# A chunked scan layer: masks move from GpSimd to VectorE, the state copy to ScalarE, two groups of loads and transposes later

## The chip, the cores and the metric

The kernel runs on one core of a Trainium2 chip. The metric is the device time of one execution in microseconds, as the median of several runs. The engines are TensorE (PE; its weight loads are listed apart as PEld), VectorE (DVE), ScalarE (ACT), GpSimd (POOL) and SyncE (SP). SP and GpSimd issue the DMA transfers of this kernel, each in the order of its own queue.

## What is computed

One layer of a latent generator, on 1024 latent and 256 context tokens with 2048 channels, in fp32. The part that matters here is a two-directional recurrence with 16 heads of 64 channels:

```python
def _rwkv_step(S, inp):
    r, w, k, v, a, b = inp
    sa = jnp.einsum('dbhvk,dbhk->dbhv', S, a)
    S = S * w[..., None, :] + sa[..., :, None] * b[..., None, :] + v[..., :, None] * k[..., None, :]
    y = jnp.einsum('dbhvk,dbhk->dbhv', S, r)
    return S, y
...
p_l = h_l @ w_in[l]                       # one input projection for all branches
S_ctx, y_c = bidir_scan(S0, *cx)          # 256 context tokens
_, y_l = bidir_scan(S_ctx, *lat)          # 1024 latent tokens
out_l = branch_output(p_l, y_l, ...)      # per-head norm of y, gates, a pooling branch, output projection
x = x + gt_l * out_l
return rms_norm(x, final_g)
```

## The kernel before

The kernel has three stages. The first (0 to about 956 us in the profile) makes the modulation, the normalised input and those columns of the input projection that the scan needs; it writes the scan's operands to DRAM (sAR, sBK, sV, sBV). The second is the scan, with the rest of the input projection woven in. The third (from about 1993 us) is the output projection with residual and norm.

The scan runs in chunks of 64 tokens. There are four groups Q of four heads and 20 chunks each (4 of context with g = 0, 16 of latent tokens), so NST = 80 steps k, each with both directions of four heads. A chunk's recurrence is solved with a triangular inverse. A step has these parts:

- `scores` (L758) multiplies the chunk's operands on TensorE into two PSUM banks, 20 steps ahead (LEAD). `masked` (L762 to L773) multiplies them with a triangular mask into the SBUF tile NM and stores it to DRAM (sNM) from GpSimd's queue. ns is 1 for context chunks (256 columns a head) and 2 for latent ones (512).
- `inverse(i)` inverts the diagonal 32x32 blocks of eight steps at once: four loads of TT from sNM (L783), then 30 pairs of VectorE instructions (L789, L791), then a store. Its first `next`, in `begin`, issues the loads. `invert` then places the pairs among the other VectorE work, and at step r = k % 8 = 4 `run_step` runs whatever is left of the inversion.
- `assemble` builds the 64x64 inverses T from these blocks (L826, L837) with one PSUM bank, B0.
- `phase_x` (L893), `phase_t` (L903), `phase_s` (L915) are the serial chain of a step. Each ends in VectorE instructions that read PSUM: Xs (L896), two SUV copies (L904, L905), and for the state St (L918) and two halves of the next step's SUV (L922). The new state Sn (L923) is made on GpSimd; the next step's `outputs` (L935, L937) and phase_s read it.
- `turned` (L881) transposes the next step's BK into bank B0, and ScalarE copies it to BKt (L882).
- `gathered` collects the outputs y. When a pair of chunks is complete in both directions, `finish` normalises it (L972 to L985), loads its gates (sBV and sG), transposes it on TensorE into bank B0 (L1001) and writes it to sM.

Between these stand `unit`s of the input projection (12 matmuls of 512 columns, L154 to L156; planned as 2.65 us), which `pump` places, and generators (`threads`: weight splits L633, gate and pooling work, `finish`), which `slot` advances. The order on TensorE, VectorE and ScalarE is the order in which the code emits the instructions; SP and GpSimd are ordered by the framework. `at["pe"]` and `at["dve"]` are the planned times of the two engines: `slot` and `invert` place VectorE work as long as `at["dve"]` is below the time that they are given. A thread that yields 0 is left until the next call of `slot`; `later()` yields 0 until one more unit has been emitted. `dense[0]` is true between phase_s of a step and the first phase of the next.

Buffers around the scan: NM, R, MR, AR, S two each, NA and SUV three, BK four, one PSUM bank for each of XU, B0, A0 and A1.

Of the kernel before, what the change touches and what calls it, by code (L numbers as in the profile page):

```python
# [11 lines left out]
ALU = mybir.AluOpType  # L12
# [47 lines left out]
def hybrid_layer_kernel(ctx: ExitStack, tc: tile.TileContext, I, out, dbg=None):  # L60
# [496 lines left out]
    with ExitStack() as p2s:  # L557
# [200 lines left out]
                    mm(ps[h][:, 64 * ns * u:64 * ns * (u + 1)], BK[hs, u // 2, u % 2, :], AR[hs, :, u // 2, u % 2, :],  # L758
                       start=True, stop=True)

        def masked(k, direct=False):
            ns = 2 if steps[k][1] else 1  # L762
            ps = scps.pop(k)
            NM = p2.tile([128, ns, 2, 4 * C], F32, tag="NM", bufs=2, name=nm("NM"))
            for h in range(2):
                nv = NM[:, :, h].rearrange("q a (u t) -> q u a t", t=C)
                pv, mv = ps[h][:, 0:256 * ns].rearrange("q (u a t) -> q u a t", u=4, a=ns), mask[:, h, :, 0:ns, :]
                if direct:
                    V.tensor_tensor(nv, pv, mv, ALU.mult)
                else:  # L770
                    S.copy(nv, pv)  # L771
                    G.tensor_tensor(nv, nv, mv, ALU.mult)  # L772
            idma(sNM[0:ns, :, :, k].rearrange("a h q u t -> q (a h) (u t)"), NM.rearrange("q a h x -> q (a h) x"))  # L773


# [131 lines left out]
        def phase_s(k):  # L907
            Q, g, s = steps[k]
            c = CCH * g + s
            SUV, S0, DY = suv[k], st["S"], bank(("DY", "B1")[k % 2])  # L910
            if c < NCH - 1:
                BKt = bkts.pop(k)
                for u in range(4):
                    for h in range(2):
                        mm(DY[hss[h], 64 * u:64 * u + 64], BKt[:, u // 2, u % 2, h, :], SUV[:, h, u // 2, u % 2, :],  # L915
                           start=True, stop=True)
                tmp = p2.tile([128, 4, C], F32, tag="St", name=nm("St"))
                V.tensor_tensor(tmp.rearrange("q u v -> q (u v)"), DY[:, 0:256], S0.rearrange("q u v -> q (u v)"), ALU.add)  # L918
                Sn = p2.tile([128, 4, C], F32, tag="S", bufs=2, name=nm("S"))
                pc = PCt[:, Q, c].rearrange("q p d -> q (p d)").unsqueeze(2).broadcast_to([128, 4, C])  # L920
                for h in range(2):
                    V.tensor_tensor(suv[k + 1][hss[h], h].rearrange("q p d v -> q (p d) v"), tmp[hss[h]], pc[hss[h]], ALU.mult)  # L922
                G.tensor_tensor(Sn, tmp, pc, ALU.mult)  # L923
                st["S"] = Sn
            if g:
                st["late"] = k, S0, DY
            else:
                suv.pop(k)
# [37 lines left out]
        def finish(Q, m, y):  # L966
            runs = (C * (6 - 2 * m), C * (8 + 2 * m))
            js = slice(2 * Q, 2 * Q + 2)
            mean = p2.tile([128, 8], F32, tag="mean", bufs=2, name=nm("mean"))
            rs = p2.tile([128, 8], F32, tag="rs", bufs=2, name=nm("rs"))  # L970
            yf = y.rearrange("q p r c v -> q (p r c) v")
            V.tensor_reduce(mean, yf, mybir.AxisListType.X, ALU.add)  # L972
            V.tensor_scalar(mean, mean, 1.0 / C, None, op0=ALU.mult)
            yield 0.7
            V.tensor_tensor(yf, yf, mean.unsqueeze(2).broadcast_to([128, 8, C]), ALU.subtract)
            sq = p2.tile([128, 8, C], F32, tag="sqy", bufs=2, name=nm("sqy"))
            S.activation(sq, yf, AF.Square)
            yield 0.7
            yield from later()
            V.tensor_reduce(rs, sq, mybir.AxisListType.X, ALU.add)  # L980
            S.activation(rs, rs, AF.Sqrt, bias=eps_ln, scale=1.0 / C)
            yield 0.6
            yield from later()
            V.reciprocal(rs, rs)
            V.tensor_tensor(yf, yf, rs.unsqueeze(2).broadcast_to([128, 8, C]), ALU.mult)  # L985
            while gates_done[0] < 2 * Q + 2:
                unit()
            parts = []
            for src in (sBV, sG):
                t = p2.tile([128, 2, 2, 128], F32, tag="bvs", bufs=2 * BVS, name=nm("bvs"))  # L990
                for r in range(2):
                    dma(t[:, :, r], src[js, :, runs[r]:runs[r] + 128].rearrange("j q t -> q j t"))
                parts.append(t)
            yield 0.8
            yield 0
            while not dense[0] and not rush[0]:
                yield 0
            ps = bank("B0")
            for i in range(8):
                for h in range(2):  # L1000
                    mm(ps[hss[h], 64 * i:64 * i + 64], yf[hss[h], i, :], ident[hss[h], hss[h]], start=True, stop=True)  # L1001
            mx = p2.tile([128, 2, 2, 128], F32, tag="mxn", bufs=2, name=nm("mx"))
            for p in range(2):
                j = 2 * Q + p
                S.activation(mx[:, p].rearrange("q r t -> q (r t)"), ps[:, 256 * p:256 * p + 256], AF.Identity,
                             bias=lbs[:, j:j + 1], scale=lgs[:, j:j + 1])
            yield from later()
            V.tensor_tensor(mx, mx, parts[0], ALU.add)  # L1008
            yield 0.7
            V.tensor_tensor(mx, mx, parts[1], ALU.mult)  # L1010
            for r in range(2):
                idma(sM[js, :, runs[r]:runs[r] + 128].rearrange("j q t -> q j t"), mx[:, :, r])
            yield 0.7
# [22 lines left out]
        def run_step(k):  # L1036
            r = k % 8
            last = k == NST - 1
            phase_x(k)
            pe(0.7, st.get("suv", 0.0))  # L1040
            xs = dve(0.41, at["pe"])
            if r in (0, 5) and k // 4 + 1 < len(batches):
                asm["now"] = assemble(k // 4 + 1)
                next(asm["now"])
            late = st.pop("late", None)
            if late:
                outputs(*late)
                pe(1.7)
            else:
                unit()  # L1050
                owed[0] -= 1
            bk_load(k + 2)
            if not last:
                step_loads(k + 1)
            if k + LEAD + 2 < NST:
                score_loads(k + LEAD + 2)
            dense[0] = False
            invert(k, max(at["pe"], xs) + 0.5)
            slot(max(at["pe"], xs) + 0.4)
            phase_t(k)  # L1060
            pe(0.7, xs)
            us = dve(0.84, at["pe"])
            if late:
                gathered(*late)
                dve(0.56)
            if k + LEAD < NST:
                scores(k + LEAD)
                pe(1.7)
            elif unit_no[0] < NU:
                unit()  # L1070
                owed[0] -= 1
            if r in (2, 7) and "now" in asm:
                run(asm.pop("now"))
                pe(0.6)
            invert(k, max(at["pe"], us) + 0.5)
            slot(max(at["pe"], us) + 0.4)
            dense[0] = True
            phase_s(k)
            pe(0.7, us)
            st["suv"] = dve(1.48, at["pe"])  # L1080
            if not last:
                turned(k + 1)
                pe(0.6)
            if k + LEAD < NST:
                masked(k + LEAD)
            if r == 4:
                i = k // 8 + 1
                if i in invs:
                    run(invs.pop(i))
                begin(i + 1)  # L1090
            n = FILLS[k + LEAD >= NST]
            left = at["pe"] + UNIT * int(owed[0] + n) + 0.7
            slot(left - 1.2)
            invert(k, left)
            pump(n)
            if r in (1, 6) and "now" in asm:
                next(asm["now"])
                pe(0.6)
# [11 lines left out]
        with tc.manual_schedule(engines={eng.PE, eng.DVE, eng.Activation}):  # L1110
            for k in range(LEAD):
                at["dve"] = max(at["dve"], at["pe"])
                scores(k, (("A0", "A1"), ("XU", "DY"))[k % 2])
                score_loads(k + 2)
                pump(1)
                masked(k, k % 2 == 0)
                if k == 9:
                    invs[0] = inverse(0)
                    next(invs[0])
                elif k > 10:  # L1120
                    for _ in range(3):
                        next(invs[0], None)
                if k == LEAD - 4:
                    bk_load(0)
                    step_loads(0)
                    bk_load(1)
# [196 lines left out]
```

## Time and profile before

| | us |
|---|---|
| runs | 2370.49, 2368.15, 2356.09 |
| median | 2368.15 |
| profiled execution, its own time | 2357.3 |
| its span, first to last instruction | 2355.5 |
| scan with look-ahead scores (steps 0 to about 59) | 1095 to 1757 |
| last twenty steps | 1757 to 1960 |

The profile records every instruction of one execution with its start and duration. A row by line gives a group of instructions: output<-inputs, shape, count, then the busy time in us, the mean of one in ns, the engine's idle time just before them, and what ended that idle time. Rows of waits name the instruction that waited, what released it, the sum in us, how often, and the longest. The granted clock of TensorE is 1.00 at 2.4 GHz and 0.50 at 1.2 GHz.

### The profile page before, as it was taken

The page shows a single profiled execution, that of the slowest core. Times are in us where ns is not written, and L with a number is a line of the kernel's source. Part 1 is how long each engine was busy: PE and PEld are TensorE (multiplying, and loading weights), DVE is VectorE, ACT ScalarE, POOL GpSimd, SP SyncE. Part 2 cuts the span into 40 slices and gives each one's busy share as a digit, 9 for nine tenths or more (in the row PEclk, how much of TensorE's full clock was granted, in tenths as well). Part 3 has the DMA queues.
Part 4 walks back from the last instruction along what each step waited for, and adds up shares of the span by engine and source line. Part 5 has one row for each costly group of instructions (what it writes and reads, how often), then busy time and mean ns, then how long its engine had stood idle before and what let it go on. Part 6 is the DMA issues. An engine that isn't in the chain of part 4 may idle for free. (4 is left out here: it accounts for less than half of the span.)

```text
span 2355.5 us, 49746 instructions
## 1 busy us (share of the span) xinstructions
PE 2155.2 (91%) x19854; PEld 1304.9 (55%) x19854; DVE 1474.1 (63%) x2544; ACT 849.3 (36%) x1447; POOL 514.0 (22%) x702
## 2 busy tenths in 40 slices
PE   2999999999999999989988989889799998999997
PEld 1445444454444444445655566556555664888886
DVE  7644756475476477456769767787586674445546
ACT  5344534344344344212223323323332223333424
POOL 3000000011000000244655555545443211000000
PEclk9999999999999999999999999999999999999999
DMA  8765555455343344796887788877877643645546
GB/s 307 232 211 171 141 146 149 140 150 154 100 127 96 104 127 112 221 299 193 249 238 226 212 237 243 258 220 231 232 232 198 187 136 104 219 130 170 192 129 206
DMA packets 494999, 437.19 MB, mean 186 GB/s; under 512 B 274328, under 2 KB 366520, under 8 KB 494512
## 3 DMA queue, kind: packets, MB, share of 16 engines
q1 hardware_dynamic: 473712, 366.88, 54.3%
q0 software_dynamic: 21056, 67.13, 8.4%
q8 instruction: 157, 2.57, 0.5%
q14 instruction: 74, 0.61, 0.1%
HBM read 316.68 MB, written 115.88 MB: 184 GB/s over the span
## 5 line engine op out<-in xcount | busy, mean ns | idle before, releaser
L154 PE MATMUL ps<-hhi,whi 128*128 128x512 f16 x1600 | 612.0, 383 | 1.6 <-DVE sg L686 0.8
L156 PE MATMUL ps<-hhi,wlo 128*128 128x512 f16 x1600 | 609.8, 381 | 0.6 <-DVE wlo L633 0.6
L155 PE MATMUL ps<-hlo,whi 128*128 128x512 f16 x1600 | 610.1, 382 | 0.0
L156 PEld LDWEIGHTS <-wlo 128*128 128x128 f16 x1888 | 185.5, 98 | 196.5 <-issue 17.5
L154 PEld LDWEIGHTS <-whi 128*128 128x128 f16 x1888 | 185.3, 98 | 192.4 <-issue 30.3
L155 PEld LDWEIGHTS <-whi 128*128 128x128 f16 x1888 | 185.8, 99 | 178.5 <-issue 21.8
L1181 PE MATMUL ps<-wolo,mhi 128*128 128x512 f32 x512 | 199.8, 390 | 2.7 <-DVE wolo L1177 2.6
L1181 PE MATMUL ps<-wohi,mlo 128*128 128x512 f32 x512 | 199.0, 389 | 0.0
L1181 PE MATMUL ps<-wohi,mhi 128*128 128x512 f32 x512 | 198.5, 390 | 0.0
L772 POOL TENSOR_TENSOR NM<-NM,mask 128x512 f32<-128x512 f32 (+1 forms) x140 | 177.8, 1288 | 54.9 <-ACT NM L771 51.0
L1177 DVE TENSOR_TENSOR wolo<-wo,wohi 128x512 fp32r<-128x512 f32 x144 | 98.2, 689 | 144.9 <-ACT wohi L1176 144.6
L147 DVE SCALAR_TENSOR_TENSOR wlo<-wraw,whi 128x512 f16<-128x512 f32 x104 | 70.6, 686 | 175.3 <-ACT whi L146 173.7
L1176 ACT CAST wohi<-wo 128x512 fp32r<-128x512 f32 x144 | 89.3, 621 | 174.6 <-PE ps L1181 156.3
L882 ACT COPY BKt<-ps 128x512 f32<-128x512 f32 x76 | 44.4, 584 | 283.3 <-PE ps L881 283.3
L896 DVE COPY Xs<-ps 128x256 f32<-128x256 f32 x80 | 33.8, 423 | 152.4 <-PE ps L893 152.1
L789 DVE TENSOR_TENSOR tm<-TT 128x30 f32<-128x30 f32 (+5 forms) x300 | 112.4, 375 | 14.0 <-DMA TT<-sNM 6.7
L923 POOL TENSOR_TENSOR S<-St,PCt 128x256 f32<-128x256 f32 x76 | 60.2, 792 | 264.4 <-DVE St L918 263.8
L791 DVE TENSOR_TENSOR TT<-TT,tm 128x30 f32<-128x30 f32 (+5 forms) x300 | 109.7, 366 | 10.3
L1181 PEld LDWEIGHTS ps<-wolo,mhi 128*128 128x128 f32 x512 | 96.1, 188 | 24.6 <-DVE wolo L1177 4.9
L1181 PEld LDWEIGHTS ps<-wohi,mhi 128*128 128x128 f32 x512 | 95.9, 188 | 21.0 <-ACT wohi L1176 1.0
L1181 PEld LDWEIGHTS ps<-wohi,mlo 128*128 128x128 f32 x512 | 96.1, 188 | 19.8
L758 PE MATMUL ps<-AR,BK 64*128 64x128 f32 (+1 forms) x1280 | 94.8, 289 | 8.2 <-issue 2.7
(232 smaller groups left out, 3523.7 us busy)
## 6 DMA issues: line engine op xcount, KB each, us to landing
wraw<-in_w_in SPq DMA_DIRECT2D x200, 256.0 KB, 3.8
BK<-sBK SPq DMA_DIRECT2D x156, 256.0 KB, 4.1
wo<-in_w_out SPq DMA_DIRECT2D x144, 256.0 KB, 2.9
sNM<-NM POOLq DMA_DIRECT2D x64, 512.0 KB, 5.4
wa<-in_w_ada SPq DMA_DIRECT2D x112, 256.0 KB, 3.3
wg<-in_w_ada SPq DMA_DIRECT2D x64, 256.0 KB, 3.0
AR<-sAR SPq DMA_DIRECT2D x64, 256.0 KB, 5.0
MR<-sNM SPq DMA_DIRECT2D x64, 256.0 KB, 3.3
```

Of the source, the lines that this page charges most:

```text
L147: V.scalar_tensor_tensor(wlo, raw, WS, whi, op0=ALU.mult, op1=ALU.subtract)
L154: mm(ps[:, :n], w[0][:, k, :], hi[kt][:, o:o + n], start=(kt == 0), stop=False)
L155: mm(ps[:, :n], w[0][:, k, :], lo[kt][:, o:o + n], start=False, stop=False)
L156: mm(ps[:, :n], w[1][:, k, :], hi[kt][:, o:o + n], start=False, stop=(kt == KT - 1))
L758: mm(ps[h][:, 64 * ns * u:64 * ns * (u + 1)], BK[hs, u // 2, u % 2, :], AR[hs, :, u // 2, u % 2, :], start=True, stop=True)
L772: G.tensor_tensor(nv, nv, mv, ALU.mult)
L789: V.tensor_tensor(tm, TT[:, 0:s, s:s + 1].broadcast_to([128, s, n]), TT[:, s:s + 1, s + 1:32].broadcast_to([128, s, n]), ALU.mult)
L791: V.tensor_tensor(TT[:, 0:s, s + 1:32], TT[:, 0:s, s + 1:32], tm, ALU.add)
L923: G.tensor_tensor(Sn, tmp, pc, ALU.mult)
L1176: S.copy(whi, raw)
L1177: V.tensor_tensor(wlo, raw, whi.bitcast(F32), ALU.subtract)
L1181: mm(banks[q, t], mix[k][m][:, tk], w, start=(k == order[0] and n == 0), stop=(k == order[-1] and n == 2))
```

## The change

`masked` always multiplies from PSUM on VectorE (before: only for every other one of the 20 steps ahead of the scan; all others were copied to SBUF by ScalarE and multiplied there by GpSimd), and enters its time in the plan. The new state Sn is no longer a product on GpSimd but two copies on ScalarE of the halves that VectorE has just written into SUV. `finish` waits for one more unit before it transposes y. The four TT loads of the next inversion are issued at r = 5, behind the scores, and no longer at the end of r = 4; the index of the inversion is the same. GpSimd keeps its DMA issues and some memsets.

```diff
-        def masked(k, direct=False):
+        def masked(k):
...
-                if direct:
-                    V.tensor_tensor(nv, pv, mv, ALU.mult)
-                else:
-                    S.copy(nv, pv)
-                    G.tensor_tensor(nv, nv, mv, ALU.mult)
+                V.tensor_tensor(nv, pv, mv, ALU.mult)
+                dve(0.35 * ns)
...
-                G.tensor_tensor(Sn, tmp, pc, ALU.mult)
+                for h in range(2):
+                    S.copy(Sn[hss[h]].rearrange("q u v -> q (u v)"), suv[k + 1][hss[h], h].rearrange("q p d v -> q (p d v)"))
...
             yield 0.8
-            yield 0
+            yield from later()
             while not dense[0] and not rush[0]:
                 yield 0
             ps = bank("B0")
...
+            if r == 5:
+                begin(k // 8 + 2)
             if r in (2, 7) and "now" in asm:
...
                 if i in invs:
                     run(invs.pop(i))
-                begin(i + 1)
...
-                masked(k, k % 2 == 0)
+                masked(k)
```

## Rows read from the trace of the kernel before

**Rows 1.** The page's head and TensorE's busy time, share and instructions.
```profile
span 2355.5 us, 49746 instructions
PE 2155.2 (91%) x19854; PEld 1304.9 (55%) x19854; DVE 1474.1 (63%) x2544; ACT 849.3 (36%) x1447; POOL 514.0 (22%) x702
```

**Rows 2.** Busy time by stage: length, PE, PEld, DVE, ACT, POOL; clock, DMA share, GB/s.
```profile
1095.00:1757.00 662.00, 581.98 (x8817) 394.59 (x8817) 490.10 (x1056) 207.10 (x408) 345.52 (x405) 0.96 0.80 232
1757.00:1960.00 203.00, 193.28 (x2739) 117.71 (x2738) 134.80 (x290) 58.79 (x107) 48.50 (x70) 1.00 0.59 164
```

**Rows 3.** TensorE's waits, 1095 to 1757 us: total, times, longest.
```profile
PE ps L915 <- DVE SUV L904: 19.3, 26, 3.0
PE ps L893 <- DMA SUV<-sV: 15.1, 8, 6.6
PE ps L1001 <- DVE y L985: 10.3, 3, 5.2
...
PE ps L903 <- DVE Xs L896: 5.6, 8, 1.0
PE ps L1001 <- ACT BKt L882: 4.4, 6, 0.7
PE ps L893 <- DVE SUV L922: 3.6, 7, 1.1
```

**Rows 4.** Busy time in the scan's eight stretches at half clock: the first, and the sum.
```profile
1213.90:1217.30 3.40, 3.40 (x11) 1.20 (x9) 1.95 (x4) 2.09 (x4) 0.83 (x1) 0.50 0.98 331
...
sum 44.30, PE 34.91 PEld 27.21 DVE 23.87 ACT 8.17 POOL 12.94; mean PE 4.36 PEld 3.40 DVE 2.98 ACT 1.02 POOL 1.62
```

**Rows 5.** The mask instruction that VectorE already has: ns min/median/max, first and last start.
```profile
L769 DVE TENSOR_TENSOR NM<-ps,mask x20: 412/679/692, 977.0 to 1058.8; 128x512 f32<-128x512 f32 x16, 128x256 f32<-128x256 f32 x4
```

**Rows 6.** The state multiply by line, 1095 to 1960 us: ns min/median/max.
```profile
L922 DVE TENSOR_TENSOR SUV<-St,PCt x152: 416/420/1000, 1096.1 to 1945.9; 64x256 f32<-64x256 f32 x152
```

**Rows 7.** VectorE's groups by line and shape, 1095 to 1757 us.
```profile
L922 DVE TENSOR_TENSOR SUV<-St,PCt 64x256 f32<-64x256 f32 x114 | 64.5, 566 | 3.6
...
L633 DVE SCALAR_TENSOR_TENSOR wlo<-wraw,whi 128x512 f16<-128x512 f32 x46 | 42.8, 935 | 0.8
...
L905 DVE COPY SUV<-ps 64x256 f32<-64x256 f32 x59 | 25.2, 428 | 1.8
```

**Rows 8.** The page's costliest groups: the same split in the first stage.
```profile
L147 DVE SCALAR_TENSOR_TENSOR wlo<-wraw,whi 128x512 f16<-128x512 f32 x104 | 70.6, 686 | 175.3 <-ACT whi L146 173.7
```

**Rows 9.** Timeline, 1581.5 to 1586.1 us: start, us, engine, line.
```profile
1580.85 0.69 DVE L1008 TENSOR_TENSOR mx<-mx,bvs 128x512 f32<-128x512 f32 x1
...
1581.58 3.33 DVE L1010 TENSOR_TENSOR mx<-mx,bvs 128x512 f32<-128x512 f32 x1
...
1581.86 2.49 POOL L772 TENSOR_TENSOR NM<-NM,mask 128x512 f32<-128x512 f32 x2
...
1586.02 0.37 PE L915 MATMUL ps<-SUV,BKt 128*64 128x64 f32 x1 [3.03 <-DVE SUV L904]
```

**Rows 10.** ScalarE's copies by line and shape, 1095 to 1757 us.
```profile
L771 ACT COPY NM<-ps 128x512 f32<-128x512 f32 x96 | 51.9, 598 | 5.5 <-issue 5.5
...
L882 ACT COPY BKt<-ps 128x512 f32<-128x512 f32 x57 | 33.3, 585 | 218.5 <-PE ps L881 218.4
...
L771 ACT COPY NM<-ps 128x256 f32<-128x256 f32 x24 | 7.9, 385 | 0.0
```

**Rows 11.** SP's queue at one r = 4, timeline 1667 to 1686 us.
```profile
1671.05 5.02 SPq L783 DMA_DIRECT2D TT<-sNM  x3
...
1679.89 1.67 SPq L856 DMA_DIRECT2D SUV<-sV  x2
```

**Rows 12.** DMA issues, 1095 to 1757 us: count, KB each, median us to landing.
```profile
SUV<-sV SPq DMA_DIRECT2D x235, 32.0 KB, 3.3
```

**Rows 13.** The TT loads (L783) by line, 1095 to 1757 us: time to landing.
```profile
DMA to landing us min/median/max: 2.8/5.0/8.2
```

**Rows 14.** Timeline, 1286 to 1288.6 us: the first of 32 transposes of y.
```profile
1288.52 0.37 PE L1001 MATMUL ps<-ident,y 64*64 64x64 f32 x2 [5.23 <-DVE y L985]
```

## The prediction

> **What bounds the kernel now.** I read the page's busy line first: TensorE is busy 91% of the span [rows 1], so time can come only from its idle tenth or from a higher clock. The busy time by stage says where that tenth lies: the steps with look-ahead scores (1095 to 1757 us, step 0 to about 59) hold 582.0 busy us of 662, the last twenty steps 193.3 of 203 [rows 2]. So some 80 us of idle TensorE lie in the first of them, and everything the change touches runs there or in the 139 us ahead of it. VectorE is at 490.1 us there, 74%, and GpSimd at 345.5. What follows the scan is bound by its own matmuls, so what the scan gains goes straight to the end.
>
> TensorE's waits in that stretch name four things worth pricing [rows 3]: copies of VectorE that come late (19.3 for phase_t's copies, 5.6 for phase_x's, 3.6 for the state written into SUV: 28.5 us together), 15.1 us for the SUV loads in 8 waits, one of them 6.6, 10.3 us for the normalised y in only 3 waits, and 4.4 us for the BKt copy in 6. Long waits also cost clock: in eight stretches the granted clock is 0.50, the 1.2 GHz level, each beginning in or just behind a wait; they last 44.3 us and TensorE is busy for 34.9 of them [rows 4]. At the full clock that work takes about half, so about 17 us hang on them.
>
> **Masks and state leave GpSimd.** Before, the 20 look-ahead steps give VectorE every other mask and the 60 later steps none. The change adds 120 masks in the stretch (96 of 512 columns, 24 of 256) and 20 before it. VectorE already did this operation from PSUM: median 0.679 us, shortest 0.412 for the 256-column form [rows 5]. So 96 x 0.68 + 24 x 0.41 = 75 us more VectorE work in 662 us.
>
> Against that stands what GpSimd costs VectorE now. The state multiply L922 has a median of 0.420 us, but a mean of 0.566 over 114 in this stretch [rows 6, 7]: 17 us. The split L633 has a mean of 0.935, while the same operation and shape on L147, where GpSimd is all but idle, has 0.686 [rows 7, 8]: 46 x 0.25 = 11 us. The same subtraction over the other groups of this stretch that read two SBUF operands (the normalisation, the pooling sums, the inversion's widest rows) gives about 32 more. VectorE instructions that read PSUM, like L905 at 0.428, do not lengthen [rows 7]. So about 60 us of VectorE's 490 come from GpSimd's computing beside it, and they go with it: 490 - 60 + 75 = 505, about 13 us more, in a stretch that I expect some 30 us shorter: 80%. VectorE's load hardly changes; its bad surprises go. One is in the timeline: L1010, normally under 0.7 us, takes 3.33 while two GpSimd masks run, and behind it phase_t's copies hold TensorE for 3.03 us [rows 9]. The order on VectorE is written by hand with planned durations (0.7 for such an instruction) in which no such delay stands; the new masks are entered at 0.35 x ns each, which is what they take.
>
> The Trainium skill, SBUF — State Buffer, section Who interferes with whom, calls this an exclusive lock on a shared port pair between GpSimd and a VectorE instruction with two SBUF inputs. By that rule the whole 60 us would go, and the trace agrees as far as the PSUM readers are unaffected.
>
> On the path I take **-15 us** of the 28.5: the long waits go, the short ones (0.4 to 1.2 us) stay, since the plan fills VectorE up to half a microsecond past TensorE's planned end. Bounds: -26 if nearly all are contention, +13 if all of VectorE's added time lies in front of copies that TensorE waits for.
>
> ScalarE loses 120 copies, 51.9 + 7.9 us [rows 10], and gets 152 copies of 64x256 from SBUF. No row shows these; the nearest are 0.385 us (256 columns from PSUM) and 0.585 (512 columns), so 58 to 89 us; I take 0.385, because the columns are the same, and ScalarE stays even. Its order matters more: the two state copies stand ahead of the BKt copy L882 and wait for L922. The chain L918, L922, L922 is 3 x 0.42 us behind phase_s's end, the second copy 0.4 more, so BKt starts about 1.1 us later than now. The next phase_s is a whole step away and hides that; the transposes of y, which need the same bank B0, do not (next part). The new state itself is read a step later. On GpSimd's queue the masks and state products, most of its 345.5 us [rows 2], disappear ahead of its DMA issues; the sNM stores have up to twenty steps of cover except for the TT loads (next part), so I count nothing here.
>
> **Diagonal block loads one step later.** At r=4 the four TT loads wait on SP's queue for the sNM store of a step that GpSimd has hardly finished. In one case they take 5.02 us there, and the SUV loads of the next step, queued behind, are issued at 1679.89 and later [rows 11]; phase_x then waits 6.6 us [rows 3]. Such a round comes every eight steps, seven of them in this stretch, and the SUV waits stand in the steps right behind them. One step later the store has long landed. The loads then sit behind the next step's SUV loads, and the step after gets its own about 2 us later (4 issues). SP is tight: 869 issues over all groups of that view, of which the SUV loads are the largest [rows 12], at about 0.6 us as in the timeline [rows 11] are some 520 of 662 us, so a little of the wait returns. New exposure: the first use of TT on VectorE is in r=6 behind phase_x, about 7 us behind the new issue point, and a load lands in 5.0 us in the median, 8.2 at most [rows 13]. Behind that use stand phase_t's copies. I take **-12 us**; bounds -15 and +9 (eight rounds late by 1.1 us with nothing gained).
>
> **Transposes of y wait for one more dense unit.** The three long waits, such as 5.23 us [rows 14], arise because the transposes are placed right behind the VectorE product that they read. With one unit of 2.65 us (planned) between, these 10.3 us go. But the thread resumes either between two units or right behind the next step's BKt transposes; in about half of the 15 sets it will be the latter, and there the wait of 0.73 (4.4 / 6 [rows 3]) becomes about 1.9: 7.5 x 1.9 = 14 against 4.4 now. Net **-1 us**; bounds -10 and +12. The loads of sBV and sG are issued before either place and move nowhere.
>
> **Clock.** If half of the stretches at 1.2 GHz disappear with their waits: **-9 us** of the 17; bounds -16 and +4.
>
> **Sum.** -15 - 12 - 1 - 9 = -37. The profiled execution took 2357.3 us (span 2355.5 and 1.8 around it), so 2320 for such an execution. It lies at the low end of the three runs (2356.09 to 2370.49, median 2368.15); for a median I add half of that distance of 10.9, and predict **2325 us**. All bounds together: 2290 to 2395 on the profiled execution's scale.
>
> **Rivals.** *The waits only change their names* (within 1%): VectorE gains nothing that TensorE sees, since its mean load is unchanged; TT lands after its first use in most of the eight rounds (+9), late SP issue keeps a third of the SUV waits, and the BKt wait takes the place of the y wait. For it: SP has little slack and every moved item lands in a tight place. Against: 3.03 and 6.6 us waits whose causes are plainly removed. That gives -15 for SUV, +5 kept, +9 for TT, -10 for the longest copies and the clock: about 2346, with the scatter 2352.
>
> *VectorE falls behind its written order* (slower): the plan now carries 1.4 us more per step, and work that finds no place is pushed together, above all the rest of an inversion, which run_step finishes in one go at r=4. If ten pairs of its instructions (about 0.75 us a pair) stand there in front of phase_x's copy, 7.5 us less the 4 us of dense units beside them: 3.5 x 8 = 28, and half a microsecond at phase_s in 60 steps is 30; less 15 from the loads: +43, 2400. It decides from the point where VectorE is busy for more than about 90% of the stretch; my sum gives 80%, which speaks against it. The Trainium skill, Perfetto Trace Analysis, section Optimizing Scalar/DVE Operations, advises giving work away from a saturated VectorE; this change does the reverse, and by that rule it would be this rival; at 74% in the trace VectorE is not saturated.
>
> **How the numbers follow.** The forecast has 0.60, the first rival 0.27, the slower one 0.13. Within 1% is about what a measurement of this kernel can tell from no change. Faster by over 1% (below 2344.5) is the forecast, within 1% the first rival, slower by over 1% (above 2391.8) the second. The range 2290 to 2385 takes in the lower bound, the forecast, the whole first rival; outside lie most of the slower case and a few in a hundred below. The forecast's own range is 2295 to 2344.
>
> **What would show it.** Right: VectorE's L922 mean at 0.42 and L633 at 0.69; no TT load waiting for sNM on SP; SUV waits under 5 us; no 3 us wait at phase_s; VectorE about 500 us busy in the scan's first sixty steps. Wrong: TensorE waiting at phase_s behind inversion instructions that wait for TT; L1001 waiting 2 us behind L882 in many sets; idle TensorE in the stretch still near 80 us. If VectorE's durations stay long without GpSimd's computing, the first step falls.

## The result

The changed kernel takes 2376.15 us (median of 20 runs), the kernel before 2360.58 us in the same comparison: a ratio of 1.0062, 95% interval 1.0049 to 1.0075. It is slower by 0.6%, where 2325 us was forecast, 1.8% below the median of 2368.15 known then. The profiled execution has a span of 2364.3 us against 2355.5 [rows 1]; it is the second fastest of its twenty (2366.07 us), so it shows 8.8 of the 15.6 us between the medians.

The profile after, first the busy time by stage (columns as in [rows 2]). The whole scan, from the first phase_x to the output projection's first matmul, is the second and third row: of the kernel before and of the changed one.

```profile
1095.00:1757.00 662.00, 572.60 (x8667) 387.07 (x8666) 473.58 (x1139) 195.66 (x392) 146.10 (x224) 0.95 0.79 230
```
```profile
1089.00:1990.10 901.10, 808.11 (x11770) 528.39 (x11769) 641.60 (x1381) 274.39 (x529) 399.39 (x482) 0.97 0.73 211
```
```profile
1082.60:1997.30 914.70, 812.09 (x11770) 529.48 (x11769) 632.50 (x1501) 287.24 (x563) 185.49 (x286) 0.96 0.72 208
```

GpSimd's computing is gone (345.5 to 146.1 us in the first stretch, what is left being memsets and DMA issues), and VectorE is busy for less time than before (632.5 against 641.6 us in the scan) although it does 120 masks more. But the scan is 13.6 us longer, and TensorE idles in it for 914.7 - 812.1 = 102.6 us against 93.0.

TensorE's waits in the changed kernel, 1095 to 1757 us, to be read beside [rows 3] (phase_t's copies are now L901, y is L983, the BKt copy L879):

```profile
PE ps L912 <- DVE SUV L901: 35.3, 23, 7.1
PE ps L999 <- DVE y L983: 19.7, 6, 4.6
...
PE ps L154 <- DVE sg L686: 6.5, 3, 2.8
PE ps L999 <- ACT BKt L879: 3.6, 2, 2.5
PE ps L823 <- ACT BKt L879: 3.0, 2, 2.7
PE ps L890 <- DMA SUV<-sV: 2.3, 3, 1.6
```

The SUV waits are gone (15.1 to 2.3). In their place stand longer waits at phase_s (19.3 to 35.3), nearly twice the y waits (10.3 to 19.7) and a wait of the dense units that was not there. What holds phase_s is in VectorE's waits of the scan:

```profile
DVE tm L786 <- DMA TT<-sNM: 24.0, 5, 6.7
```

VectorE waits for the late TT loads, and phase_t's copies are queued behind. The largest of them in the timeline, one fence for VectorE and TensorE:

```profile
1224.02 0.42 DVE L893 COPY Xs<-ps 128x256 f32<-128x256 f32 x1 [1.81 <-PE ps L890]
...
1231.13 0.20 DVE L786 TENSOR_TENSOR tm<-TT 128x30 f32<-128x30 f32 x1 [6.68 <-DMA TT<-sNM]
...
1233.18 0.41 DVE L901 COPY SUV<-ps 64x256 f32<-64x256 f32 x1
...
1233.73 0.45 PE L912 MATMUL ps<-SUV,BKt 128*64 128x64 f32 x2 [7.11 <-DVE SUV L901]
```

The clock adds to it. The scan's stretches at a granted clock of 0.50 sum up as follows (first the changed kernel's, then those of the kernel before, the eight of [rows 4] and one ahead of them):

```profile
sum 71.90, PE 60.79 PEld 40.14 DVE 43.82 ACT 18.23 POOL 9.06; mean PE 4.05 PEld 2.68 DVE 2.92 ACT 1.22 POOL 0.60
```
```profile
sum 47.70, PE 38.31 PEld 30.49 DVE 24.29 ACT 8.56 POOL 16.20; mean PE 4.26 PEld 3.39 DVE 2.70 ACT 0.95 POOL 1.80
```

TensorE does 60.8 us of its work at 1.2 GHz instead of 38.3. If half of the difference is lost to it, that is 11 us, an estimate. The rows themselves show less: of the 13.6 us, 9.6 are idle time and 4.0 are busy time (808.1 to 812.1). So TensorE's other work was about 7 us shorter in this execution, and no run here says why.

### The profile page after: what moved, and what is told of

Same layout as the page of the kernel before. It is cut to its first block, busy times and chain, and to the rows that moved or that the text cites. A ratio compares the mean times of both kernels' runs of the same rounds, so it can differ in the third digit from the quotient of the medians.

```text
span 2364.3 us, 49649 instructions
## 1 busy us (share of the span) xinstructions
PE 2158.9 (91%) x19854; PEld 1307.2 (55%) x19854; DVE 1468.2 (62%) x2684; ACT 853.0 (36%) x1461; POOL 275.7 (12%) x486
## 4 chain that ended last, share of the span: by engine, by line
PE 35%; DVE 10%; DMA 3%; issue 2%; SPq 1%; ACT 1%; POOL 0%; DVEq 0%; ACTq 0%; POOLq 0%
PE ps L1180 14%; PE ps L154 4%; PE ps L155 4%; PE ps L156 4%; DVE tm L786 2%; PE ps L890 2%; DMA TT<-sNM 1%; DVE TT L788 1%; PE ps L878 1%; PE ps L912 1%; PE ps L823 1%; PE ps L684 1%; PE ps L900 1%; DVE SUV L919 1%; DVE SUV L902 1%
## 5 line engine op out<-in xcount | busy, mean ns | idle before, releaser
L921 ACT COPY S<-SUV 64x256 f32<-64x256 f32 x152 | 61.3, 403 | 290.1 <-DVE SUV L919 288.2
L786 DVE TENSOR_TENSOR tm<-TT 128x30 f32<-128x30 f32 (+5 forms) x300 | 98.7, 329 | 30.8 <-DMA TT<-sNM 24.0
L768 DVE TENSOR_TENSOR NM<-ps,mask 128x512 f32<-128x512 f32 (+1 forms) x160 | 94.5, 632 | 26.2 <-PE ps L758 14.9
L788 DVE TENSOR_TENSOR TT<-TT,tm 128x30 f32<-128x30 f32 (+5 forms) x300 | 99.5, 332 | 10.3
L770 POOL DMA_DIRECT2D sNM<-NM x80 | 60.2, 752 | 382.9 <-DVE NM L768 334.6
```

The costliest lines, as they stand in the source:

```text
L786: V.tensor_tensor(tm, TT[:, 0:s, s:s + 1].broadcast_to([128, s, n]), TT[:, s:s + 1, s + 1:32].broadcast_to([128, s, n]), ALU.mult)
L788: V.tensor_tensor(TT[:, 0:s, s + 1:32], TT[:, 0:s, s + 1:32], tm, ALU.add)
L921: S.copy(Sn[hss[h]].rearrange("q u v -> q (u v)"), suv[k + 1][hss[h], h].rearrange("q p d v -> q (p d v)"))
```

## The experiments

The theory at the start: the later TT loads cost more than they bring (A). Its rival: the masks' entry in VectorE's plan forces other work together (B). Both were partly wrong, and a third cause came up. Ratios are to the kernel before, with their 95% intervals. Single executions differ by about 1% and their scans start anywhere from 1080.7 to 1097.1 us, so verdicts go by the ratios, and the profiles tell only where the waits are.

**e1, the TT loads back at r = 4.**
```diff
-            if r == 5:
-                begin(k // 8 + 2)
...
+                begin(i + 1)
```


> The changed kernel with the four TT loads put back to the end of r = 4; masks, state copy and later transposes stay. Theory A (the later loads cost more than they bring): in the changed kernel VectorE waits 24.0 us in 5 waits for TT to land, and behind them TensorE waits 25 us at phase_s in five waits of 2.1 to 7.1 us, with the clock at 0.50 behind most of them. These go, so about 25 us less than the changed kernel, a ratio to the kernel before of about 0.995 to 1.000; the SUV waits come back only in part (2.3 us in the changed kernel, 15 before), since the masks reach DRAM sooner without the GpSimd products. Rival B (the masks on VectorE and their plan entry cost the time, by forcing other work together): the ratio stays within 0.3% of the changed kernel's 1.006.


Measured: 1.0055 [1.0038, 1.0073], no clear difference from the change. TensorE's waits in its scan:
```profile
PE ps L999 <- DVE y L983: 20.8, 6, 4.8
PE ps L890 <- DMA SUV<-sV: 18.1, 7, 6.0
PE ps L154 <- DVE sg L686: 14.0, 4, 9.5
...
PE ps L912 <- DVE SUV L901: 10.8, 20, 0.9
```
The TT waits are gone and phase_s waits fall to 10.8, but the SUV waits are back, and more than before. On SP's queue the TT loads now wait 2.3 us in all for their store, 1.3 at most, where they waited 8.1 us in the kernel before, up to 4.8 at a time, and yet the SUV loads are late. What stands ahead of them on the queue is the issuing of the TT loads itself. TensorE's longest SUV wait, 6.0 us, lies behind this round (the issues first, then the only wait of the queue from 1503 to 1513 us):
```profile
1505.17 6.95 SPq L780 DMA_DIRECT2D TT<-sNM  x3
1512.16 1.33 SPq L853 DMA_DIRECT2D SUV<-sV  x2
```
```profile
SPq L780 <- DMA wraw<-in_w_in: 1.4, 1, 1.4
```
Three loads hold SP for almost 7 us, of which 1.4 are a wait. Theory A had the trade wrong: what the later place costs and what it brings are about equal here.

**e2, the transposes of y back; e3, loads and transposes back** (masks, state copy and plan entry remain). e2's edit, which e3 has beside that of e1:
```diff
-            yield from later()
+            yield 0
```


> The changed kernel with the transposes of y as before (they resume at the next slot, not behind one more unit). TensorE waits for y went from 10.3 us in 3 waits to 19.7 us in 6, against what the later place was meant to do. Theory A: the later place pushes each normalisation thread further back, so that more of them are still open when a later one forces them to the end in one go, with the transposes right behind their operand; undone, the y waits fall to 10 us or less, and the ratio to about 1.001 to 1.004. Rival B: the forcing comes from the fuller plan of VectorE (0.7 us a mask entered), not from the later place; then the y waits stay near 20 us and the ratio near 1.006.

> Both moves undone: only the masks on VectorE (with plan entry) and the state copy on ScalarE remain. Theory A (the move off GpSimd is a gain, the two later places are the loss): no TT wait on VectorE, phase_s waits of about 10 us in all where the kernel before has 23, y waits about 10: ratio 0.985 to 0.993. Rival B (the move itself is the loss): ratio 1.002 or more.


Measured: e2 1.0120 [1.0097, 1.0143], e3 1.0070 [1.0047, 1.0093]. Without the later transposes e2 is 0.6% worse than the change; with the loads at r = 4 (e1 to e3) the difference is not clear. The y waits are as large without the later transposes: 20.8 us in e2, 21.3 in e3. They come from something else. In e3 phase_s waits fall to 11.9 us from 19.3 in the kernel before, with the loads where they were: the shorter waits that were forecast from GpSimd's absence are there, and are eaten by longer ones for y, dense units and BKt.

**e4, the change without the plan entry.**
```diff
-                dve(0.35 * ns)
```


> The changed kernel without entering the masks' time in the plan of VectorE; every mask still runs there. Theory A (the TT loads are the main loss): the TT waits stay (20 us or more), and the ratio stays at 1.00 to 1.01. Rival B (the plan entry forces work together): y waits fall from 19.7 to about 10, the waits for gate and output work (7.3 and 1.9 us) vanish, and the ratio falls to 0.998 or less; against that, VectorE is then overfilled by up to 1.4 us a step, and phase_s waits in many steps grow.


Measured: 1.0031 [1.0012, 1.0050]. TensorE's first rows of waits, and the TT wait on VectorE:
```profile
PE ps L911 <- DVE SUV L900: 46.0, 27, 8.4
...
PE ps L998 <- ACT BKt L878: 11.9, 7, 2.5
...
PE ps L822 <- ACT BKt L878: 4.1, 3, 1.9
```
```profile
DVE tm L785 <- DMA TT<-sNM: 24.0, 6, 8.0
```
Not one y wait is left. The TT waits stay, and the waits on BKt grow, up to 2.5 us each, because the transposes of y now really come right behind the BKt transposes: in TensorE's order 7 sets of 16 do, where 3 did in the changed kernel.

**f1, f2: the TT loads on GpSimd's queue**, at r = 5 and at r = 4, with the plan entry; **f3: f2 without the entry.**
```diff
-                    dma(TT[p0:p0 + 32], sNM[0, h, r0:r0 + 32, ...
+                    idma(TT[p0:p0 + 32], sNM[0, h, r0:r0 + 32, ...
```


> The changed kernel with only the queue of the four TT loads changed: GpSimd's, at the same place (r = 5). Putting the loads back on SP to r = 4 took the 24 us of TT waits away but brought 18.2 us of SUV waits back although no TT load waited for a store on SP any more; so the theory now is that the place in SP's queue matters, behind loads that wait for buffers (R behind L935, AR and BK behind L758). Theory A (SP's queue): off that queue the loads land before their first use; TT waits fall from 24.0 us to under 6, SUV waits stay under 5, phase_s waits fall from 37 to about 13; ratio 0.992 to 0.999. Rival B (five microseconds of landing time are too late at r = 5 on any queue): TT waits stay at 15 us or more and the ratio at 1.003 or more.

> As the run before, but the TT loads at the end of r = 4 again, on GpSimd's queue. Theory A: no TT wait and no SUV wait of more than 3 us in all; what remains is the y waits of about 20 us and the clock; ratio 0.990 to 0.998, no more than 0.3% from the run before. Rival B (the loads' own traffic delays the SUV loads, whatever the queue): SUV waits of 10 us or more come back, ratio 1.002 or more.

> As the run before, and the masks' time is not entered in VectorE's plan. Without that entry the changed kernel had no y wait at all (19.7 with it), 0.8 us instead of 7.3 in front of dense units, and phase_s waits of 47.8 us, 24 of them behind TT. Theory A: with TT on time phase_s waits are about 24 us, y waits none: ratio 0.985 to 0.995, faster than the run before by 0.2% or more. Rival B (without the entry VectorE is overfilled, and phase_s pays all of what y gains): within 0.2% of the run before or slower.


Measured: f1 1.0094 [1.0079, 1.0109], f2 1.0070 [1.0049, 1.0091], f3 0.9986 [0.9967, 1.0004]. VectorE's TT wait in f1:
```profile
DVE tm L786 <- DMA TT<-sNM: 23.3, 6, 6.9
```
So r = 5 is too late on either queue, and f1 is even 0.3% slower than the change. On GpSimd's queue the reason is another one, the wait for the stores of sNM (1095 to 1757 us):
```profile
POOL TT L780 <- DMA sNM<-NM: 15.8, 6, 5.4
```
In f2 the TT and SUV waits are both small (1.8 and 6.0 us), yet the kernel is no faster than e1: 21.0 us of y waits remain, and 81.7 us of TensorE's work at half clock. f2's scan, with the columns of the third row of the result:
```profile
1095.80:2007.70 911.90, 820.77 (x11768) 535.55 (x11768) 632.75 (x1501) 287.02 (x563) 209.17 (x318) 0.95 0.73 209
```
TensorE idles for 91.1 us, less than the 93.0 of the kernel before; what is longer is its busy time, 820.8 against 808.1. Removing the plan entry alone (f2 to f3) brings 0.8%: no y wait, and 57.1 us at half clock.

**f4, g1, g2: one part each on the kernel before.** f4 has the later TT loads, g1 the later transposes, g2 the plan entry while the masks stay on ScalarE and GpSimd, so that not one instruction is added:
```diff
                     G.tensor_tensor(nv, nv, mv, ALU.mult)
+                dve(0.35 * ns)
             idma(sNM[...
```


> The kernel before with the later TT loads alone (masks still on ScalarE and GpSimd). Theory A (the place in SP's queue makes TT late whatever the masks do): VectorE waits 15 us or more for TT, SUV waits fall from 15.2 to under 6; ratio 1.002 to 1.010. Rival B (it is the shorter steps or the fuller queues of the changed kernel that make TT late): TT waits under 5 us and a ratio of 0.993 to 0.998.

> The kernel before with the later transposes of y alone. Theory A (the later place does what it was meant to, where the plan leaves room): y waits of 10.3 us fall below 3, the waits on the BKt copy stay near 5.8; ratio 0.992 to 0.998. Rival B (the later place itself pushes the normalisation threads into forced runs): y waits of 15 us or more, ratio 1.001 or more.

> The kernel before with the masks' time entered in VectorE's plan (0.7 us for each of two latent masks), though the masks stay on ScalarE and GpSimd: not one instruction is added, only the order changes. Theory A (the fuller plan alone forces the threads together): y waits rise from 10.3 to about 20 us, waits of dense units for gate and output work to 7 us or more, more time at half clock; ratio 1.004 to 1.010. Rival B (it takes the masks on VectorE as well): y waits stay at 10 us, ratio 0.998 to 1.002, or lower since emptier slots leave phase_s's copies more room.


Measured: f4 1.0045 [1.0027, 1.0062], g1 0.9995 [0.9972, 1.0018], g2 1.0096 [1.0065, 1.0127]. g2's waits on TensorE:
```profile
PE ps L1002 <- DVE y L986: 23.0, 6, 6.1
PE ps L916 <- DVE SUV L905: 15.4, 24, 1.4
...
PE ps L154 <- DVE sg L686: 7.1, 4, 3.5
PE ps L684 <- DVE sg L678: 4.8, 2, 3.1
```
The entry alone costs 1% on the kernel before, more than the whole change: the y waits go from 10.3 us to 23.0, and the dense units wait for the output work as in the changed kernel. That is what the slower rival of the prediction describes, at another place than it named. How it comes about is in the timeline of the changed kernel, where one normalisation runs as a block between phase_t's copies and the scores:
```profile
1275.48 0.43 DVE L902 COPY SUV<-ps 64x256 f32<-64x256 f32 x1
...
1275.92 0.49 DVE L957 TENSOR_TENSOR y<-ps,y 128x128 f32<-128x128 f32 x2
...
1276.33 0.68 DVE L978 TENSOR_REDUCE rs<-sqy 128x8 f32<-128x512 f32 x1
...
1277.37 0.20 DVE L982 RECIPROCAL rs<-rs 128x8 f32<-128x8 f32 x1 [0.37 <-ACT rs L979]
1277.61 0.69 DVE L983 TENSOR_TENSOR y<-y,rs 128x512 f32<-128x512 f32 x1
...
1278.45 1.83 PE L999 MATMUL ps<-ident,y 64*64 64x64 f32 x29 [4.62 <-DVE y L983]
```
When the third and the fourth `finish` of a group begin, `gathered` calls `settle(fins[-3])`, and at the first latent chunk of the next group it settles what is left. That sets `rush`, under which `later()` does not wait: the rest of the thread is emitted in one go, transposes included.

How often that happens can be counted in the traces. Transposes of y directly behind phase_t's matmuls come from such a forced run, since `dense[0]` is false there and only `rush` lets them through. Of 14 to 16 sets that each trace shows, 3 stand there in the kernel before, 7 with the entry alone (g2), 8 in the changed kernel and 4 in the changed kernel without the entry (e4). In the changed kernel 18.5 of its 19.7 us of y waits stand in front of these eight sets. So the entry doubles the forced runs, with the masks on VectorE and without. The code says how: with 1.4 us more in the plan per step, `slot` finds `at["dve"]` beyond its limit earlier, and threads advance less. The planned times themselves were not recorded.

f4's VectorE waits 14.5 us for TT, and its SUV waits vanish, at +0.45%. g1 removes the y waits (none of that kind is left), but its SUV waits are 25.3 us against 15.1: given back at once.

**g3, masks and state copy alone, without the entry; g4, f3 with the state copies behind the BKt copy on ScalarE.** g4's edit to f3:
```diff
-                for h in range(2):
-                    S.copy(Sn[hss[h]]..., suv[k + 1][hss[h], h]...)
...
                 turned(k + 1)
                 pe(0.6)
+            if "copy" in st:
+                Sn, nxt = st.pop("copy")
+                for h in range(2):
+                    S.copy(Sn[hss[h]]..., nxt[hss[h], h]...)
```


> Only the masks on VectorE and the state copy on ScalarE, without the plan entry; loads, transposes of y and the order of all other work as in the kernel before. Theory A (moving the work off GpSimd is a gain in itself): phase_s waits at or under 23 us, since GpSimd no longer delays VectorE, SUV waits at or under 15; ratio 0.990 to 0.998. Rival B (the 75 us more on VectorE, unplanned, stand in front of phase_t's copies): phase_s waits of 30 us or more, ratio 1.000 or more.

> The kernel with the TT loads on GpSimd's queue at r = 4 and no plan entry (ratio 0.9986), with the two state copies placed behind the BKt copy on ScalarE. Theory A (the copies hold up BKt, as the prediction said): the waits on BKt in front of the transposes of y and of assemble fall from 11.9 and 4.4 us to about 6 and 2, with less time at half clock; ratio 0.990 to 0.996. Rival B (BKt is late because its own transposes come late): these waits stay, ratio 0.997 to 1.000.


Measured: g3 1.0034 [1.0015, 1.0053], with 14.3 us of waits of the transposes on BKt as its largest row; g4 0.9907 [0.9881, 0.9932], 2336.1 us. g4's waits on TensorE, and its sum at half clock:
```profile
PE ps L889 <- DMA SUV<-sV: 17.3, 6, 4.7
PE ps L911 <- DVE SUV L900: 13.4, 21, 1.9
...
PE ps L997 <- ACT BKt L878: 5.0, 7, 0.7
```
```profile
sum 37.50, PE 36.63 PEld 28.11 DVE 21.26 ACT 3.11 POOL 3.77; mean PE 4.07 PEld 3.12 DVE 2.36 ACT 0.35 POOL 0.42
```
The waits of the transposes of y on BKt fall from 11.9 us in 7 to 5.0 in 7, the longest from 2.5 to 0.7, and the work at half clock from 57.1 us in f3 to 36.6, worth 10 us by the same estimate; TensorE's busy time in the scan fell as much, from 812.7 to 802.4 us. In the change's own order the two copies stand ahead of BKt:
```profile
1235.63 0.63 PE L878 MATMUL ps<-ident,BK 128*128 128x128 f32 x2
1235.71 0.87 DVE L919 TENSOR_TENSOR SUV<-St,PCt 64x256 f32<-64x256 f32 x2
1236.24 0.83 ACT L921 COPY S<-SUV 64x256 f32<-64x256 f32 x2 [12.91 <-DVE SUV L919]
...
1237.09 0.58 ACT L879 COPY BKt<-ps 128x512 f32<-128x512 f32 x1
```

**h1 to h4: what each part costs where the others do not act.** h1 is the changed kernel with g4's order on ScalarE; h2 is g3 with it; h3 is g4 with the TT loads back on SP at r = 4; h4 is h3 with them at r = 5, that is the changed kernel without the entry and with the copies behind BKt. Each is a combination of edits shown above.

> The changed kernel with the two state copies behind the BKt copy on ScalarE; plan entry and later TT loads stay. Theory A (three separate losses that add up): the waits on BKt fall from 5.7 and 5.1 us to about 3 and 2, the y waits (19.7) and TT waits (24) stay; ratio 1.000 to 1.004, below the changed kernel's 1.0062. Rival B (the order on ScalarE costs only where the plan entry is gone and transposes follow the BKt copy more often): ratio within 0.2% of 1.0062.

> Masks on VectorE and state copy on ScalarE alone, no plan entry, copies behind the BKt copy; TT loads and transposes of y as in the kernel before. Theory A (moving the work off GpSimd is a gain once its order on ScalarE is right): phase_s waits about 16 us against 23 before, waits on BKt about 6, ratio 0.990 to 0.997. Rival B (no gain of its own; the 0.9907 came from the loads' queue and the later transposes): ratio 0.998 or more.

> The fastest kernel so far (ratio 0.9907) with the TT loads back on SP's queue, at r = 4. Theory A (on SP they displace the SUV loads): SUV waits of 20 us or more against 17.3; ratio 0.993 to 0.998. Rival B (the queue does not matter): within 0.2% of 0.9907.

> As the run before, with the TT loads at r = 5 behind the scores as in the changed kernel; so this is the changed kernel without the plan entry and with the copies behind BKt. Theory A (the later place costs by itself): VectorE waits 15 us or more for TT, SUV waits under 5; slower than the run before by 0.3 to 0.8%. Rival B (its cost needs the fuller plan): within 0.2% of the run before.

| kernel | loads | plan entry | copies | ratio | interval |
|---|---|---|---|---|---|
| changed | SP, r = 5 | yes | before BKt | 1.0062 | 1.0049 to 1.0075 |
| h1 | SP, r = 5 | yes | behind | 1.0023 | 0.9999 to 1.0046 |
| e4 | SP, r = 5 | no | before BKt | 1.0031 | 1.0012 to 1.0050 |
| h4 | SP, r = 5 | no | behind | 0.9953 | 0.9932 to 0.9973 |
| h3 | SP, r = 4 | no | behind | 0.9952 | 0.9930 to 0.9973 |
| g4 | GpSimd, r = 4 | no | behind | 0.9907 | 0.9881 to 0.9932 |
| h2 (y as before) | SP, r = 4 | no | behind | 0.9982 | 0.9963 to 1.0002 |

The order on ScalarE costs 0.4% in the changed kernel (h1) and 0.8% without the entry (e4 to h4); the entry costs 0.3% (e4) and 0.7% (h1 to h4). Neither alone is the loss; with both removed (h4) the change is 0.5% faster than the kernel before, 11 us of the 37 that were forecast. The later TT loads are worth nothing either way there: h4 shows phase_s waits of 46.1 us with 18.5 of VectorE's waits named for TT and 13.1 more put down to other transfers at the same instruction, h3 shows SUV waits of 24.6 us instead, and the ratios are equal. h2 says that the move off GpSimd with the right order on ScalarE is at most a small gain by itself; g4 has it beside the later transposes and TT off SP's queue.

## Why the prediction was wrong, step by step

- **Masks on VectorE, GpSimd gone, -15: the waits went as priced, the time did not follow.** Groups of VectorE and ScalarE in the changed kernel, 1095 to 1757 us, beside [rows 5] and [rows 7]:
```profile
L768 DVE TENSOR_TENSOR NM<-ps,mask 128x512 f32<-128x512 f32 x94 | 60.6, 686 | 1.4
...
L919 DVE TENSOR_TENSOR SUV<-St,PCt 64x256 f32<-64x256 f32 x112 | 47.0, 420 | 3.6
L921 ACT COPY S<-SUV 64x256 f32<-64x256 f32 x112 | 45.1, 403 | 223.5 <-DVE SUV L919 222.1
...
L633 DVE SCALAR_TENSOR_TENSOR wlo<-wraw,whi 128x512 f16<-128x512 f32 x44 | 29.8, 684 | 0.2
```
  The state multiply is back at 0.420 us, the split at 0.684, a mask takes 0.686. VectorE's busy time in the scan fell from 641.6 to 632.5 us with 72 us of masks added, so about 81 went where 60 were forecast for the first sixty steps. (In that sum 505 is 15 us more than 490, not 13; nothing hangs on it.) e3 shows phase_s waits of 11.9 us, and phase_x's and the state's rows nearly gone, so about 15 us of these waits went. But h2, which has this part alone without the entry and with the better order on ScalarE, is at 0.9982 with an interval up to 1.0002: at most 9 us. Its SUV waits are 19.7 us against 15.1.
- **"The new masks are entered at 0.35 x ns each, which is what they take": the first step that failed.** The duration is right, and I gave the entry no cost. But the plan decides which threads are forced, and the entry takes these from 4 to 8. It costs 0.3% in the change (e4), 0.7% with the other order on ScalarE (h1 to h4), and 1.0% on the kernel before (g2), where it stands for masks that VectorE does not do. The slower rival named the mechanism, work pushed together for want of a place, but looked for it in the inversion and gave it 0.13. Its condition, VectorE busy for over 90%, was not needed: it is busy for 473.6 us of 662, 72%.
- **Diagonal block loads, -12 with a bound of +9: the gain was right, the exposure mis-sized.** SUV waits fell from 15.1 to 2.3 us, and VectorE then waited 24.0 us for TT. I took the four loads to be issued together about 7 us ahead of their use. On SP's queue of the changed kernel they are not:
```profile
1216.12 0.77 SPq L780 DMA_DIRECT2D TT<-sNM  x1
1216.99 1.85 SPq L863 DMA_DIRECT2D MR<-sNM  x1
...
1219.40 1.93 SPq L780 DMA_DIRECT2D TT<-sNM  x1
1221.43 1.63 SPq L747 DMA_DIRECT2D BK<-sBK  x1
...
1223.58 2.21 SPq L780 DMA_DIRECT2D TT<-sNM  x2
```
  The last two go out 7.5 us behind the first and half a microsecond before phase_x's copy at 1224.02. Between them stand four other loads, two of which wait 0.9 and 1.3 us for their buffers, and a TT load that takes 1.93 us to issue. The SUV loads were no longer held up, but the -12 did not come: e1 and the change, and h3 and h4, show no clear difference.
- **"The four TT loads wait on SP's queue for the sNM store": misread.** The 5.02 us of [rows 11] are no such wait. From 1669 to 1678.5 us the kernel before has one wait on SP's queue, and it is not for a store:
```profile
SPq L747 <- PE ps L893: 0.5, 1, 0.5
```
  The loads took that long to issue, one of them 3.5 us, and the SUV wait of 6.6 us followed. Waits for the store did occur in other rounds (8.1 us in four). But in e1 they are 2.3 us in all and the SUV waits 18.1, the longest behind TT loads that are slow to issue. Nor has the store "long landed" one step later: in the changed kernel TT loads wait 4.6 us for it, in four waits.
- **Transposes of y, -1: right alone, wrong in company.** On the kernel before, the later place removes all y waits (g1). In the change the forced runs pass it by, and the waits rise to 19.7.
- **BKt 1.1 us later: right in size, and its price too small.** I put 14 us of waits against 4.4. In the changed kernel only three sets follow the BKt transposes; e4 shows 11.9 us in seven, 1.7 each where 1.9 was forecast. Not in the sum were assemble's waits on BKt and the clock behind all of these: moving the copies (f3 to g4) took away 6.9 us of waits in front of the transposes of y and 2.9 in front of assemble's, SUV waits rose by 13.9, and still TensorE's busy time fell by 10.3 us with less work at half clock. The order alone costs 0.4 to 0.8%.
- **Clock, -9: wrong in sign.** The work at half clock rose by 22.5 us, about +11 by the estimate of the prediction; TensorE's busy time in the scan rose by 4.0. The longest wait at phase_s went from 3.0 to 7.1 us.
- **SP is tight** was right: several times when a wait elsewhere went, SUV waits came up (g1 25.3, h3 24.6, g4 17.3 us against 15.1).
- **The rivals.** By the prediction's own bands 0.6% slower is the first rival's, within 1%, to which it gave 0.27. Of that rival's terms TT behind its first use came true; the SUV waits did not stay, and the loss through the plan is not among them. So the time falls in its band by a mechanism that is in part another.

What stays open: whether the slow issues are all of the reason why the TT loads at r = 4 cost 0.4% more on SP than on GpSimd's queue (h3 to g4), and why with the other causes present (e1 to f2) the queue makes no difference that can be told. The loads of h3 and of g4 (ns min/median/max):
```profile
L779 SPq DMA_DIRECT2D TT<-sNM x28: 325/695/5255, 1129.3 to 1673.4; - x28
```
```profile
L779 POOL DMA_DIRECT2D TT<-sNM x32: 784/799/1348, 1129.2 to 1746.6; - x32
```
The SUV waits differ by 7.3 us, the kernels by about 10. Open too is why one such load takes 0.3 us to issue on SP and another 5.3, and how much of a difference between two single profiles is the executions' own scatter.

## What to carry to other kernels

Where an order is written by hand from a planned clock, the planned duration is itself a knob: a true entry can cost time by itself (0.3 to 0.7% here), because it decides what is forced together later. Before moving work onto an engine with an in-order queue, look at what is queued behind it there (here the BKt copy behind two state copies), and put the instruction with the nearest reader first. A load that is moved later needs its slack measured from the last of its transfers on that queue to the first use, not from its place in the code. A long row of a DMA queue is a wait only if the queue's waits say so; it can be the issuing itself.

## What the runs showed of the hardware

- The sum of TensorE's waits does not tell what they cost in clock. f2 idles less in its scan than the kernel before (91.1 against 93.0 us) and does 81.7 us of work at the granted clock of 0.50 against 38.3. In the changed kernel TensorE waits from 1226.6 to 1233.7 us; the granted clock falls to 0.50 at 1230.3 and rises again at 1237.2. Which waits make the clock fall, and which do not, was not taken apart.
- On SP's queue a load of the same 128 KB took 0.3 to 3.5 us to issue in the kernel before and up to 5.3 in h3; on GpSimd's queue the same loads took 0.8 to 1.3 us (g4).
- With GpSimd's products gone, the state multiply takes 0.416 to 0.424 us in the scan, where it took up to 1.000 before [rows 6], and L1008, the line that was L1010, 0.691 to 0.693, where one took 3.33 before [rows 9]. The Trainium skill, SBUF — State Buffer, section Who interferes with whom, calls the cause an exclusive lock; the trace agrees, in that this excess went with GpSimd's products while its DMA issues stayed.
- A ScalarE copy of 64x256 from SBUF takes 0.403 us, near the 0.385 of 128x256 from PSUM.
